# A two-batch encoder layer: held-back copies, other DRAM rows, low parts on one engine, longer score runs, and a list schedule that passes work over

## The chip, the cores and the metric

The kernel runs on one core of one Trainium2 chip. The metric is the device time of one execution in microseconds (us), as the median of several runs. A profiled execution gives the span (first to last instruction), the busy times of the engines and every instruction with its start.

The engines are TensorE (PE in the profile; its weight loads are PEld), VectorE (DVE), ScalarE (ACT), GpSimd (POOL) and SyncE (SP), which here issues all DMA transfers from one queue in program order.

## The reference

One layer of an encoder is applied to a prompt (512 tokens) and to a sample (1024 tokens) with the same weights, in float32, model width 1024. Cut to what matters:

```python
h = rmsnorm(x, norm_g)
qa, ka, va, za, qb, kb, vb, zb, ga, gb = split(h @ w_in)   # 4*512, 512,128,128,512, 1024,1024
qa, ka, qb, kb = (rmsnorm per head of 64)
oa = neighbourhood_attention(qa, ka, va, rpb_a) * silu(za)      # 8 heads, 8 x 16 window of the grid
ob = window_gqa_attention(qb, kb, vb, t5_table, sink_b) * silu(zb)  # 8 heads, 2 key heads, |i-j| <= 128
merged = sigmoid(ga) * (oa @ w_o_a) + sigmoid(gb) * (ob @ w_o_b)
y = x + merged @ w_out
```

## The kernel before

**Products.** Every float32 product is made of three float32r products. An operand is split into a high part (ACT copies it with rounding, line 1172) and a low part (the rest, by a subtraction on DVE or POOL, line 1177); the three products are high x high, high x low and low x high (lines 764 for the attention's projections, 1293 to 1295 elsewhere). The large products of the dense phases are partly done with Strassen-like sums of blocks: the sums of activations for the sample, called T, are made early, stored in the DRAM tensor `t_d`, read back at the start of the sample's dense phase into the tiles U, fh and w32, and split into the tiles T.

**Stages.** Normalization of the prompt; attention of the prompt; dense phase of the prompt, which also normalizes the sample; attention of the sample; dense phase of the sample. An attention phase runs six groups: four of branch A (two heads each) and two of branch B (four heads each). In a group each tile of 128 tokens (4 in the prompt, 8 in the sample) is projected with 24 products of 384 columns into a bank "p" of PSUM (two of these); squares are summed (`sq`, `ss`), POOL makes the factors (`rs_v`, `rs_r`, lines 795 and 802), DVE scales q and k (`qk`, line 819), PE transposes them (line 864) into a bank "x" (five of these). In group A the projection reads the activations directly; in group B it reads copies `hb` in another token order, four tiles of [128, 4, 128] a projection, made by ACT or DVE (lines 665 and 667).

`attend` collects blocks of 128 queries. A batch of them (two in A, one in B) is one operation of PE, the score run: for each block and pair of heads six products on 64 rows (line 937), two heads side by side on the two halves of the array, each head with its own "x" bank. `weigh` then adds bias and takes the maximum (line 972, DVE), the exponential (line 981, ACT), the scaling, transposes of the weights (line 1029), their split (`pp`) and the products with v (line 1066). The output tile `ot` goes to DRAM: in A one store of summed halves, in B two stores (one for each half e of the partitions) into `o_d[e, 4..7]` with 128 tokens in a row.

**Dense phases.** z products (`post_z` multiplies silu(z) with the attention's output read back from DRAM; for branch B two loads `ot`, added), gate products, the products with w_o and with w_out. Products that need nothing from the attention are also offered to PE during it: whole gate products on bank "d" (`fill_gates`, 3 in the prompt and 8 in the sample, in DRAM afterwards), and in the sample the first halves of four z products (`kept_z`, i = 0 to 3), where from i = 1 the second half waits for the attention's last exponential (`exps_done`).

**Order.** All operations are given to a planner (`Flow`) with the engines that may run them, estimated durations, a priority and what they wait for. A tile's work has the priority of its tile's number, the sample's attention 100 more; the next group's weights are three tiles ahead of their use, bias tables one. `run` is a list schedule: whenever an engine is free it takes the most urgent operation that is ready, has buffers, and would not be done sooner elsewhere; this fixes the order of instructions of each engine before the kernel is compiled. On the chip every engine goes through its list in order and waits on semaphores. In the sample's attention durations on ACT, DVE and POOL are planned 1.1 times longer (`slack`); the work of the dense phases has slack 1.

## Time and profile before

| | us |
|---|---|
| median of 3 runs | 1133.49 (1132.47 to 1138.85) |
| profiled execution, its own time | 1135.29 |
| its span | 1133.5 |
| PE busy | 1119.0 |
| DVE busy | 860.1 |
| ACT busy | 651.9 |
| POOL busy | 337.3 |

The granted clock of TensorE is 1.0 (its 2.4 GHz level) over the span. In the trace the prompt's attention ends at about 217 us, its dense phase at 400, the sample's attention at 787, its dense phase at the end. A matmul's row is its start and a modelled duration; since matmuls are pipelined, what one costs is read from the distance between starts. DMA share is the mean busy share of the core's 16 DMA engines.

### The profile page before, as it was taken

To read this page: it belongs to the slowest core of one execution; us is meant where nothing else is said; L and a number is where in the kernel's file an instruction comes from. 1 tells how busy PE (TensorE), PEld (TensorE's weight loads), DVE (VectorE), ACT (ScalarE), POOL (GpSimd) and SP (SyncE) were. 2 spreads that over 40 slices of the span, in tenths; PEclk is the share of its full clock that TensorE was granted. 3 is DMA by queue.
4 is the path that set the end of the run, shared out by engine and by line. 5 is a ranking of instruction groups with operands and counts; after the bars stand their busy time and mean duration, and the time that the engine had idled before them with its cause. 6 is when DMAs were issued, how large, how long until landed. Compare 5 with 4: busy or idle time off the path is not lost.

```text
span 1133.5 us, 18690 instructions
## 1 busy us (share of the span) xinstructions
PE 1119.0 (99%) x6079; PEld 973.2 (86%) x6079; DVE 860.1 (76%) x1988; ACT 651.9 (58%) x1499; POOL 337.3 (30%) x438
## 2 busy tenths in 40 slices
PE   8999999999999999999999999999999999999998
PEld 6999988888888889999999988988788888888887
DVE  5888797587776568787878888885988766677764
ACT  6777987644432257565769888876543335423430
POOL 4653433000011154434324344420333322222211
PEclk9999999999999999999999999999999999999999
DMA  7854543488886732121212314244977645867862
GB/s 263 276 155 138 184 115 103 110 257 248 256 278 216 254 128 91 27 63 30 82 41 85 81 38 112 57 131 121 307 241 234 224 156 170 281 207 222 280 215 93
DMA packets 139108, 186.11 MB, mean 164 GB/s; under 512 B 29897, under 2 KB 68561, under 8 KB 139010
## 3 DMA queue, kind: packets, MB, share of 16 engines
q1 hardware_dynamic: 139010, 184.91, 51.8%
q8 instruction: 48, 0.79, 0.3%
q14 instruction: 50, 0.41, 0.1%
HBM read 137.66 MB, written 51.92 MB: 167 GB/s over the span
## 4 chain that ended last, share of the span: by engine, by line
PE 93%; DMA 2%; DVE 2%; issue 1%; ACT 1%; POOL 1%; SPq 0%; DVEq 0%; ACTq 0%
PE p L764 25%; PE x L1294 9%; PE x L1295 9%; PE x L1293 9%; PE x L1066 5%; PE x L937 5%; PE x L1029 5%; PE d L1293 4%; PE d L1295 4%; PE d L1294 4%; PE p L1294 4%; PE p L1295 4%; PE p L1293 4%; PE x L864 2%; DMA w<-in_w_att_dram 1%
## 5 line engine op out<-in xcount | busy, mean ns | idle before, releaser
L764 PE MATMUL p<-whi,hh 128*128 128x384 f32 x384 | 133.4, 348 | 0.0
L764 PE MATMUL p<-whi,hl 128*128 128x384 f32 x384 | 132.2, 344 | 0.0
L764 PE MATMUL p<-wlo,hh 128*128 128x384 f32 x384 | 131.8, 343 | 0.0
L1172 ACT ACTIVATE whi<-raw 128x512 fp32r<-128x512 f32 (+1 forms) x140 | 81.4, 600 | 71.2 <-PE x L1294 22.3
L981 ACT ACTIVATE sb<-sb,mx 128x384 f32<-128x384 f32 (+1 forms) x192 | 107.8, 565 | 16.9 <-DVE mx L972 16.5
L1295 PE MATMUL x<-T,wlo 128*128 128x512 f32 x280 | 108.9, 389 | 0.0
L1294 PE MATMUL x<-T,whi 128*128 128x512 f32 x280 | 108.9, 389 | 0.0
L1293 PE MATMUL x<-T,whi 128*128 128x512 f32 x280 | 108.9, 389 | 0.0
L764 PE MATMUL p<-whi,hb 128*128 128x384 f32 x384 | 107.6, 346 | 0.0
L1177 POOL TENSOR_TENSOR wlo<-raw,whi 128x512 fp32r<-128x512 f32 (+1 forms) x33 | 39.5, 1204 | 215.6 <-DMA raw<-in_w_g_dram 112.9
L1040 DVE TENSOR_TENSOR pp<-x,pp 128x512 fp32r<-128x512 f32 (+1 forms) x136 | 82.5, 638 | 19.6 <-ACT pp L1035 19.0
L1177 DVE TENSOR_TENSOR wlo<-raw,whi 128x512 fp32r<-128x512 f32 (+1 forms) x107 | 72.0, 682 | 32.3 <-ACT whi L1172 28.7
L802 POOL TENSOR_TENSOR rs_r<-rs_v,mhalf 128x4 f32<-128x4 f32 (+1 forms) x72 | 80.5, 1118 | 5.7
L1035 ACT ACTIVATE pp<-x 128x512 fp32r<-128x512 f32 (+1 forms) x136 | 70.8, 559 | 15.8 <-PE x L1029 14.3
L1294 PE MATMUL x<-hl,whi 128*128 128x512 f32 x200 | 77.8, 389 | 0.0
L1295 PE MATMUL x<-hh,wlo 128*128 128x512 f32 x200 | 77.8, 389 | 0.0
L1293 PE MATMUL x<-hh,whi 128*128 128x512 f32 x200 | 77.8, 389 | 0.0
L1066 PE MATMUL x<-pp,v 128*128 128x256 f32 (+1 forms) x368 | 75.8, 322 | 0.0
L764 PEld LDWEIGHTS p<-whi,hl 128*128 128x128 f32 x384 | 72.6, 189 | 1.3 <-issue 1.0
L764 PEld LDWEIGHTS p<-wlo,hh 128*128 128x128 f32 x384 | 72.7, 189 | 1.0 <-issue 0.7
L764 PEld LDWEIGHTS p<-whi,hh 128*128 128x128 f32 x384 | 72.7, 189 | 0.7 <-DVE v L812 0.3
L764 PEld LDWEIGHTS p<-whi,hb 128*128 128x128 f32 x384 | 69.1, 188 | 3.1 <-issue 1.3
(388 smaller groups left out, 2965.1 us busy)
## 6 DMA issues: line engine op xcount, KB each, us to landing
raw<-in_w_g_dram SPq DMA_DIRECT2D x84, 256.0 KB
w<-in_w_att_dram SPq DMA_DIRECT2D x46, 384.0 KB
raw<-in_w_z_dram SPq DMA_DIRECT2D x40, 256.0 KB
ot<-o_d SPq DMA_DIRECT2D x36, 256.0 KB
g_d<-C SPq DMA_DIRECT2D x34, 256.0 KB
fr<-in_w_g_dram SPq DMA_DIRECT2D x28, 256.0 KB
raw<-in_w_out_dram SPq DMA_DIRECT2D x28, 256.0 KB
out_dram<-C SPq DMA_DIRECT2D x19, 256.0 KB
```

What stands on the lines that cost most here:

```text
L764: pe.matmul(ps.t[:, :GW], part[u](k), mv.t[:, c], start=k == 0 and m == 0, stop=k == KC - 1 and m == 2,)
L802: lambda e: nc.gpsimd.tensor_tensor(r.t[:, :nn], rv.t[:, :nn], mhalf[:, :nn], op=ALU.pow),
L937: pe.matmul(pss[2 * pair + i].t[:, :width], q.t[rows, u, at : at + P], kv[:, tiles[0] : tiles[-1] + 1 : step], start=n == 0, stop=n == 2,)
L981: act.activation(sb.t[:, :width], sb.t[:, :width], AF.Exp, bias=mx.t[:, i : i + 1], scale=-1.0, accum_out=sm.t[:, i : i + 1],)
L1035: lambda e, pt=pt, pp=pp, nn=nn: act.activation(pp.t[:, 0, :nn], pt.t[:, :nn], AF.Copy),
L1040: lambda e, pt=pt, pp=pp, nn=nn: dve.tensor_tensor(pp.t[:, 1, :nn], pt.t[:, :nn], pp.t[:, 0, :nn].bitcast(F32), op=ALU.subtract),
L1066: pe.matmul(out(), v.t[:, vs], mv(), start=first, stop=last)
L1172: (("act", ACT_(n)),), lambda e: act.activation(hi(), src(), AF.Copy), prio,
L1177: lambda e: engines[e].tensor_tensor(lo(), src(), hi().bitcast(F32), op=ALU.subtract), prio,
L1293: pe.matmul(out, hi.t[:, cs], mh(), start=first and k == 0, stop=False, **more)
L1294: pe.matmul(out, hi.t[:, cs], ml(), start=False, stop=False, **more)
L1295: pe.matmul(out, lo.t[:, cs], mh(), start=False, stop=last and k == len(ws) - 1, **more)
```

## The change

Six edits.

- Copies: the four `hb` copies of a B projection also wait until the projection six tiles earlier has begun. Only the first four of a phase were free to run earlier than that.
- DRAM rows: A outputs keep four rows of `o_d`; B outputs go to a new tensor `ob_d`, ordered as the z products read them. A load of 256 KB for the z product of B reads rows of 512 tokens (2 KB). In the sample each B block is stored with four transfers of pieces of 64 tokens (256 bytes) instead of two of 128 tokens (512 bytes); in the prompt the pieces keep their size.
- Low parts: for the sums read from `t_d` and the weights of the sample's first z pair (priority 0), the low parts are made on DVE only.
- Score runs: in the prompt's A groups a batch has four blocks instead of two, so it waits for the group's last tile. The second block of each two shares the banks of the first, at column 256.
- Late z products: the products of `kept_z` with i = 2 and 3 wait for the attention's last product with v (`f.weighed`).
- Patience: with `expect` the planner notes when each operation whose last input has been started will be ready. With `sooner` ACT, DVE and POOL pass over an operation with priority 90 or more and slack other than 1 (so the sample's attention) if an operation more urgent by over 3 will be ready within half its duration.

```diff
+PATIENT = ("act", "dve", "pool")
+URGENT = 3
+SHARE = 0.5
+FROM = 90
+AHEAD = 6
...
+        def expect(o, end):
+            for x in o.outs:
+                x.open -= 1
+                x.eta = max(x.eta, end + min(self.LAG.get((o.eng, e), 100) for e, _ in x.choice))
+                if not x.open and x.eta > now:
+                    coming[x.choice[0][0]].append(x)
+
+        def sooner(o, e, ns):
+
+            if e not in PATIENT or o.prio < FROM or o.slack == 1:
+                return False
+            coming[e] = [x for x in coming[e] if x.eta > now and x.eng is None]
+            t = [x.eta for x in coming[e] if x.prio < o.prio - URGENT and x.eta < now + SHARE * ns]
+            if t:
+                at(min(t), 4, None)
+            return bool(t)
...
-                        if all(room(v, n) for v, n in o.new) and not any(locked(v, e) or v.held and not v.t for v in o.vals) and not barred(o, e) and all(
+                        if all(room(v, n) for v, n in o.new) and not any(locked(v, e) or v.held and not v.t for v in o.vals) and not barred(o, e) and not sooner(o, e, ns) and all(
...
-    o_d = {geo.nt: dpool.tile([2, 8, P, geo.nt], F32, tag=f"o_d{geo.nt}", name=f"o_d{geo.nt}") for geo in (gp, gs)}
+    o_d = {geo.nt: dpool.tile([4, P, geo.nt], F32, tag=f"o_d{geo.nt}", name=f"o_d{geo.nt}") for geo in (gp, gs)}
+    ob_d = {geo.nt: dpool.tile([geo.nt // 512, 2, 8, 64, 512], F32, tag=f"ob_d{geo.nt}", name=f"ob_d{geo.nt}") for geo in (gp, gs)}
...
-                            prio - 1, new=[hb[m][q]], hold=[v], after=[o for u in h_ops.values() for o in u], port=True,
+                            prio - 1, new=[hb[m][q]], hold=[v], port=True,
+                            after=[*(o for u in h_ops.values() for o in u), f.begun[nt, prio - AHEAD]],
...
+            shared = br == "A" and nt == NT_P
...
-                pss = [bank("x") for _ in range(nh)]
+                second = shared and len(states) % 2
+                pss = [(v, 256) for v, _ in states[-1][2]] if second else [(bank("x"), 0) for _ in range(nh)]
...
+                                ps, a = pss[2 * pair + i]
                                 pe.matmul(
-                                    pss[2 * pair + i].t[:, :width], q.t[rows, u, at : at + P],
+                                    ps.t[:, a : a + width], q.t[rows, u, at : at + P],
...
+            f.weighed = o
...
-                for e in range(2):
-                    dst = o_d[nt][e, 4 + 2 * g : 6 + 2 * g, :, runs[0][0] : runs[0][0] + P]
-                    dst = dst.rearrange("c (i d) n -> d (c i) n", d=64)
...
+                m, t = 512 // nb, runs[0][0] // P
+                for n in range(nt // 512):
+                    for e in range(2):
+                        dst = ob_d[nt][n, e, 4 * g : 4 * g + 4, :, t * m : t * m + m].rearrange("a p m -> p a m")
+                        o = sp(
+                            lambda n=n, e=e, dst=dst: nc.sync.dma_start(dst, ot.t[e * 64 : e * 64 + 64, :, n * m : n * m + m]),
+                            1024 * m, prio, use=[ot],
+                        )
...
-                size = 2 if br == "A" else 1
+                size = 1 if br == "B" else 4 if nt == NT_P else 2
...
-        def split(hi, lo, src, n, prio, new_hi, new_lo, src_v, after=()):
+        def split(hi, lo, src, n, prio, new_hi, new_lo, src_v, after=(), both=True):
...
-                any_tt(n),
+                any_tt(n)[: 1 + both],
...
-                        (vh, k == 0), (vl, k == 0), [st],
+                        (vh, k == 0), (vl, k == 0), [st], both=d is m_d,
...
-            w = weight_tiles([*first, s2, s3, s1, raw[1, 1], s4], 6, prio - 0.5)
+            w = weight_tiles([*first, s2, s3, s1, raw[1, 1], s4], 6, prio - 0.5, prio > 0)
...
-                    src = o_d[nt][e, c].rearrange("p (i n) -> p i n", n=P)[:, :, a // nb : a // nb + m]
-                    dst = lambda ot=ot: ot.t[:, :n].rearrange("p (i n) -> p i n", n=m)
+                    src = ob_d[nt][a // nh, e].rearrange("(c i) p n -> c (i p) n", i=2)[c - 4, :, :n]
...
-            o = product(ps, ws[0], mov_h(0, 0), i / 4 - 1, True, True)
+            o = product(ps, ws[0], mov_h(0, 0), i / 4 - 1, True, True, [f.weighed] if i > 1 else [])
```

## Rows read from the trace of the kernel before

**Rows 1.** The page, part 1: busy us (share of the span) and instructions of each engine

```profile
PE 1119.0 (99%) x6079; PEld 973.2 (86%) x6079; DVE 860.1 (76%) x1988; ACT 651.9 (58%) x1499; POOL 337.3 (30%) x438
```

**Rows 2.** Busy by stretch: PE, PEld, DVE, ACT, POOL; then clock, DMA share, GB/s

```profile
600.00:650.00 50.00, 50.00 (x330) 45.57 (x328) 43.41 (x123) 45.85 (x106) 20.51 (x26) 1.00 0.28 80
...
800.00:820.00 20.00, 18.18 (x77) 13.76 (x75) 19.29 (x25) 11.06 (x21) 7.34 (x5) 1.00 0.96 308
```

**Rows 3.** Waits of PE over the span: us in total, times, longest us

```profile
PE x L864 <- DVE qk L819: 3.1, 3, 1.8
```

**Rows 4.** PE in order of time: start, us, line, tiles; round two score runs

```profile
63.43 0.34 PE L764 MATMUL p<-whi,hl 128*128 128x384 f32 x1
63.60 0.34 PE L764 MATMUL p<-whi,hh 128*128 128x384 f32 x1
63.87 0.97 PE L937 MATMUL x<-kt,qt 64*128 64x256 f32 x12
64.78 0.45 PE L764 MATMUL p<-wlo,hh 128*128 128x384 f32 x1
65.06 0.34 PE L764 MATMUL p<-whi,hl 128*128 128x384 f32 x1
...
740.31 1.33 PE L937 MATMUL x<-kt,q 64*128 64x384 f32 x12
```

**Rows 5.** Line 937 alone: count, duration ns min/median/max, first and last start; prompt's A

```profile
L937 PE MATMUL x<-kt,qt x96: 271/278/384, 38.5 to 127.6; 64*128 64x256 f32 x96
```

**Rows 6.** All engines in order of time, start of the sample's attention

```profile
402.23 1.31 POOL L1177 TENSOR_TENSOR fl<-fr,fh 128x512 fp32r<-128x512 f32 x1 [11.40 <-ACT fh L1172]
...
402.62 2.15 DVE L667 CAST hb<-hl 128x512 fp32r<-128x512 f32 x2
...
403.62 1.22 POOL L795 TENSOR_SCALAR rs_v<-ss 128x4 f32<-128x4 f32 x1
...
406.02 0.19 POOL L795 TENSOR_SCALAR rs_v<-ss 128x4 f32<-128x4 f32 x1
...
406.45 0.44 PE L864 MATMUL x<-ident,qk 128*128 128x128 f32 x2 [1.84 <-DVE qk L819]
```

**Rows 7.** Busy by stretch (columns as in rows 2), start of the sample's dense phase

```profile
796.00:798.00 2.00, 2.00 (x10) 1.65 (x10) 2.00 (x6) 1.97 (x5) 0.00 (x0) 1.00 1.15 296
...
804.00:806.00 2.00, 2.00 (x10) 1.69 (x9) 1.92 (x4) 2.00 (x5) 0.00 (x0) 1.00 1.01 371
```

**Rows 8.** SP's issues in order of time, end of the attention and after

```profile
785.75 1.24 SPq L1102 DMA_DIRECT2D o_d<-ot__10494  x2
...
793.90 3.66 SPq L1520 DMA_DIRECT2D u_d<-C  x1
...
804.60 3.58 SPq L1520 DMA_DIRECT2D u_d<-C  x1
```

**Rows 9.** DVE and POOL in order of time, low parts of T and of weights

```profile
805.83 0.69 DVE L1177 TENSOR_TENSOR T<-w,T 128x512 fp32r<-128x512 f32 x1
...
810.76 1.71 POOL L1177 TENSOR_TENSOR wlo<-raw,whi 128x512 fp32r<-128x512 f32 x1
811.27 1.75 DVE L1177 TENSOR_TENSOR T<-w,T 128x512 fp32r<-128x512 f32 x1
```

**Rows 10.** PE in order of time, T products of the first z pair

```profile
811.11 0.40 PE L1293 MATMUL d<-T,whi 128*128 128x512 f32 x1
813.08 0.50 PE L1294 MATMUL d<-T,whi 128*128 128x512 f32 x1 [1.57 <-DVE T L1177]
...
820.67 0.50 PE L1294 MATMUL p<-T,whi 128*128 128x512 f32 x1 [0.65 <-DVE T L1177]
```

**Rows 11.** PE in order of time, end of the sample's attention

```profile
784.00 1.10 PE L1066 MATMUL x<-pp,v 128*128 128x512 f32 x4
...
786.32 0.39 PE L1293 MATMUL x<-hh,whi 128*128 128x512 f32 x1
786.54 0.39 PE L1294 MATMUL x<-hl,whi 128*128 128x512 f32 x1
```

More of the change, by code (lines that the diff above doesn't have):

```diff
@@ L137 @@
 class Op:
-    __slots__ = ("choice", "emit", "new", "vals", "after", "outs", "prio", "left", "lag", "key", "eng", "port")
+    __slots__ = ("choice", "emit", "new", "vals", "after", "outs", "prio", "left", "lag", "key", "eng", "port", "slack", "open", "eta")
 class Flow:
@@ L210, in run @@
         for o in self.ops:
-            o.left = len(o.after)
+            o.left = o.open = len(o.after)
+            o.eta = 0
             for a in o.after:
@@ L258, in barred @@
             return True
+        coming = {e: [] for e in ready}
+        def expect(o, end):
[12 more added lines that the diff above has]
+            return bool(t)
         def backlog(e, item):
@@ L300, in run @@
                         at(dma_free + 950, 2, got)
+                    expect(got, dma_free + 950 if got.lag else now + ns)
             if not events:
@@ L947, in attend @@
             o = f.op(
-                (("pe", ns),), emit, prio, new=[v for _, _, pss, sbs in states for v in (*pss, *sbs)],
+                (("pe", ns),), emit, prio, new=[v for _, _, pss, sbs in states for v in (*(ps for ps, a in pss if not a), *sbs)],
                 use=[queries(block) for block in batch], after=[o for b in batch for t in b[1] for o in info[t][2]],
@@ L967, in weigh, with score, emit @@
             mx, sm, rs, es = sums
-            def score(i, ps, sb):
-                def emit(e, i=i, ps=ps, sb=sb):
+            def score(i, ps, a, sb):
+                def emit(e, i=i, ps=ps, a=a, sb=sb):
                     init = 3.0e38 if br == "A" else nsink[:, 4 * g + i : 4 * g + i + 1]
                     dve.tensor_tensor_reduce(
-                        out=sb.t[:, :width], in0=ps.t[:, :width], in1=bias_of(br, nb_t, i, table), scale=1.0,
+                        out=sb.t[:, :width], in0=ps.t[:, a : a + width], in1=bias_of(br, nb_t, i, table), scale=1.0,
                         scalar=init, op0=ALU.add, op1=ALU.min, accum_out=mx.t[:, i : i + 1],
@@ L990, in score @@
                 x.vals = [*x.vals, mx]
-            for i, (ps, sb) in enumerate(zip(pss, sbs)):
-                score(i, ps, sb)
+            for i, ((ps, a), sb) in enumerate(zip(pss, sbs)):
+                score(i, ps, a, sb)
             if br == "B":
@@ L1088, in emit @@
                     if len(runs) == 1:
-                        dst = over(o_d[nt][0, g], runs).rearrange("(i p) n -> p i n", i=2)
+                        dst = over(o_d[nt][g], runs).rearrange("(i p) n -> p i n", i=2)
                         nc.sync.dma_start(dst, ot.t[:64, ::2])
@@ L1092, in emit @@
                     for i in range(2):
-                        dst = over(o_d[nt][0, g, 64 * i : 64 * i + 64], runs)
+                        dst = over(o_d[nt][g, 64 * i : 64 * i + 64], runs)
                         nc.sync.dma_start(dst, ot.t[:64, 2 * i].rearrange("p (a b) -> p a b", b=64))
@@ L1258, in load_raw, with weight_tiles @@
             return v
-        def weight_tiles(operands, per, prio):
+        def weight_tiles(operands, per, prio, both=True):
             n = -(-len(operands) * 4 // per)
@@ L1275, in weight_tiles @@
                         lambda src=src, sc=sc: src.t[:, sc], m * P, prio,
-                        (hi, ti not in seen), (lo, ti not in seen), [src],
+                        (hi, ti not in seen), (lo, ti not in seen), [src], both=both,
                     )
@@ L1529, in post_z @@
                 if c < 4:
-                    src, dst = o_d[nt][e, c, :, a : a + n], lambda ot=ot: ot.t[:, :n]
+                    src = o_d[nt][c, :, a : a + n]
                 else:
-                    src = o_d[nt][e, c].rearrange("p (i n) -> p i n", n=P)[:, :, a // nb : a // nb + m]
-                    dst = lambda ot=ot: ot.t[:, :n].rearrange("p (i n) -> p i n", n=m)
+                    src = ob_d[nt][a // nh, e].rearrange("(c i) p n -> c (i p) n", i=2)[c - 4, :, :n]
                 dma(
-                    lambda dst=dst, src=src: nc.sync.dma_start(dst(), src), 512 * n, prio - 0.5, new=[ot],
+                    lambda ot=ot, src=src: nc.sync.dma_start(ot.t[:, :n], src), 512 * n, prio - 0.5, new=[ot],
                     after=o_stores[c, a // nh],
```

9 lines of the change are left out of this document (2 added, 7 removed).

## The prediction

> **What bounds the kernel now.** I began with the busy shares of the page: TensorE (PE) is busy 1119.0 of 1133.5 us [rows 1]. The profiled execution took 1135.29 us, 1.8 us more than its span, and the median of the runs is 1133.49 us; I take the sum in the span and subtract it from the median. In the stretch 600 to 650 us, the second half of the sample's attention, PE is busy 50.00 of 50, with ScalarE (ACT) at 45.85 and VectorE (DVE) at 43.41 [rows 2]: the code gives PE products there that nobody waits for yet (gate products on the bank "d", then the first z products), and they fill every gap. So moving DVE or ACT work changes nothing by itself. Only two things shorten this kernel: fewer PE cycles, or less of the 14.5 us in which PE stands still.
>
> Where does it stand still? The change can reach two causes: in the list of waits the transposes of line 864 wait for `qk` of line 819, 3.1 us in three places, longest 1.8 [rows 3], and in the order of time a product stands 1.57 us at once for the low part of a T sum (line 1177) [rows 10]. The head, waiting for its first loads, and the drain at the end hold most of the rest and are not touched. The stretch 800 to 820 shows PE at 18.18 of 20 while the DMA engines are at 0.96 and DVE at 19.29 [rows 2]: this is the start of the sample's dense phase, where the stored sums T are read from DRAM.
>
> **The change part by part.**
>
> Score runs. The score products (line 937) work on 64 rows, all others on 128. The last 128-row product before a run starts at 63.60, the run at 63.87, the next product at 64.78 and the one after at 65.06 [rows 4]. Undisturbed neighbours start 0.17 us apart (63.43, 63.60). From 63.60 to 65.06 are 1.46 us; two ordinary starts take 0.35 of it, so the run costs 1.11. How much of that is switching? A run of the same 12 products with 384 columns takes 1.33 where 256 columns take 0.97 [rows 4]: 0.36 for six concurrent pairs of 128 more columns, 0.06 a pair, so 256 columns are worth 0.12 a pair and six pairs 0.72. What is left, 0.39, is the way in and out of the mode. The prompt's A groups hold 96 such products [rows 5], eight runs of 12. Four blocks in one batch make four runs of 24. Gain 4 x 0.39 = **1.6 us** of PE time. Ends: 1.6, and nothing if the bunching makes as much idle time: the run now waits for the fourth tile, then eight score operations come to DVE at once, and four of the five "x" banks are held twice as long. The cover is the next group's projections (two "p" banks) and the gate products; I take 1.6, since PE is never idle in that part of the trace.
>
> Copies. The B projections read a copy of the activations (`hb`, four buffers). Nothing keeps the first four copies of a phase from running as soon as an engine is free, and in the sample they do so at 402 us: DVE takes two from 402.62, 2.15 us [rows 6]. They are first read in group B, four A groups later. Beside them POOL's `rs_v` of the first A tile takes 1.22 us, where the next one, with no copy beside it, takes 0.19. It sits on the chain ss, rs_v, rs_r, qk, and PE waits for it until 406.45, idle 1.84 [rows 6]. Held back until the projection six tiles earlier has begun, the copies run in the fourth A group instead, where PE does not wait for ACT or DVE. Gain 1.22 - 0.19 = **1.0 us**. Ends: 1.84, if the second tile's chain, delayed by ACT's copies, is part of the wait; nothing, because POOL is also busy with a gate weight's low part until 403.54 [rows 6] and a new order can put more there. In the prompt they go the same way, from a place where PE is covered: nothing.
>
> DRAM rows. For z columns of branch B in the sample, each load of `o_d` gathers 1024 pieces of 256 bytes, two loads a product. In the stretch 796 to 798, where these pass, the DMA engines move 296 GB/s at a share of 1.15; in 804 to 806 371 at 1.01 [rows 7]: 257 against 367 per full share. A load of 256 KB thus costs 1.02 instead of 0.71 us; as rows of 2 KB each saves 0.3. Four pass before the last T load: 1.2 us of a saturated DMA. And directly behind each such pair SP sits in the issue of one small store for 3.66 and 3.58 us [rows 8], with the T loads (U, fh, w) queued behind; without the small pieces this block should go. Against it: the stores of the last B block become four issues instead of two, and two cost 1.24 us [rows 8]. The T loads stand behind them on SP, so they start 1.24 later. For the first T sums these two about cancel: 0. For the last four T loads, issued behind the second block, two blocks of 3.6 are gone: they are no longer late, and the waits for the parts made of them go, 1.2 us in two late starts, the last at 820.67 with 0.65 of idle [rows 10].
>
> Low parts. In the sample's first z pair, and for the T sums, POOL may take low parts. While POOL runs one (1.71 at 810.76), DVE's T low part takes 1.75, where an undisturbed one takes 0.69 [rows 9]; PE waits for exactly this one: it starts a product at 811.11 and the next only at 813.08 [rows 10], 1.97 instead of 0.22 [rows 11], a loss of 1.75. With all on DVE, behind 808.4 there are five low parts (two more T, the two weights that POOL had, and T's last) of 0.69: 3.45, or 4.1 with the `ot` sum between; T's last ends at 811.8 to 812.5 instead of 813.02. Gain 0.5 to 1.2, I take 0.8.
>
> Together the dense start has 1.75 + 1.4 (three further late starts between 809 and 821, the last of them the one at 820.67) = 3.1 us to give; from the two edits I take 0.8 + 1.2 = **2.0 us**. Ends: 3.1, and nothing if PE only runs into the next missing operand, DVE being at 19.29 of 20.
>
> Late z products. Products i = 2 and 3 now wait for the last value product of the attention. Before, that product is at 784.00 and the first of i = 2 already follows it, at 786.32 [rows 11]. So the edit moves nothing in the old order: 0. It only keeps them as cover for the T loads should the order change.
>
> Patience. In the sample's attention an ACT, DVE or POOL operation is passed over if one at least three tiles more urgent is to be ready within half its duration. It shortens the chains that free banks, but PE is covered there (50.00 of 50 [rows 2]), so what it gains comes out only as fill kept for the dense start, already counted to its end. Ends: 1 us gained, and 1 lost in idle slices; I take 0.
>
> Sum: 1.6 + 1.0 + 2.0 = 4.6 us of 1135.29, so 1130.7 for a profiled execution, and **1128.9 us** as median.
>
> **The rivals.**
>
> 1. Only the mode switches are saved. The dense start stays bound by DMA (shares 1.15 and 1.01 [rows 7]) and DVE, and the wait for `qk` moves to another operation. For it: one late operand there is followed by the next in the rows. Against: SP's two blocks are plainly from the small pieces. 1133.49 - 1.6 = 1131.9.
>
> 2. All that can close closes: 1.6 + 1.84 + 3.1, and 0.9 of the other `qk` waits: 7.4, so 1126.1. For it: fill exists at each place; against: a new order has small waits of its own.
>
> 3. Slower: fill runs out before the attention ends. Before, all z products not held back were used up at 786.32, 1.4 us after the last value products, which start at 784.00 and take four starts of 0.23 [rows 11]. Holding back i = 2 and 3 takes 10.6 us (48 products of 0.22) away from that cover. If patience leaves ACT or DVE (43 to 46 of 50 [rows 2]) idle for 0.35 us twice in each of the group B tiles, 16 tiles, the chain grows 11.2, PE stands 9.8, and 4.6 is given back: 1138.7. It is slower than before from a growth of 6.0 us on. Against it: weights, bias tables and the first copies are nearly the only operations three tiles ahead.
>
> 4. The small stores bite. Each B block of the sample now stores 256-byte pieces. With the 1.24 us of issue not cancelled and 0.3 for the slower rate of such pieces, T is late by 1.5: gain 3.1, 1130.4. The Trainium skill, page "DMA: Bandwidth & Descriptors", section Specifications, wants at least 512 bytes for line rate and names a read-modify-write below it, which speaks against this edit. The trace of before shows 256-byte pieces as loads only, and no row can show what a store of them costs.
>
> **How the numbers follow.** Forecast 0.46 (1128.9, own range 1126.8 to 1131); rivals 1 to 4: 0.22, 0.14, 0.08, 0.10. The range for 8 in 10 goes from rival 2's side, 1125.5, to past rival 1 with one microsecond or two of new waits, 1134.5; rival 3 is left out. A measurement of this kernel tells about 0.5% from no change, 5.7 us. Faster by more: rival 2 and a third of the forecast, 0.30. Slower by more: over half of rival 3, 0.05. Within: 0.65.
>
> **What the profile after should show.** Prompt score runs of 24 products, four of them, with the same 0.39 around each. No `hb` copy near 402; `rs_v` there at 0.19; PE's wait for `qk` at that place 0.8 or less. No SP issue over 2 us near 794 and 805; loads of `ob_d` with 2 KB rows; four B stores a block. No T low part on POOL, T low parts of 0.69 on DVE, and PE idle in 800 to 825 falling from 2.5 to under 1 us. PE's busy time lower by 1.6 at most. I am wrong if PE shows idle time before the last value product (rival 3), if its idle time is 13 us or more in spite of the steps (rival 1), or if new waits stand in the prompt between 38 and 110 us, where the runs come late.

## The result and the profile after

The changed kernel takes 1140.22 us (median; 1137.51 to 1144.49) where the kernel before took 1134.79 beside it: 1.0050 times as long, 95% interval 1.0032 to 1.0068. It is slower by half a per cent, 5.7 us past the upper end of the range that was given. The profiled execution took 1140.18 us, with a span of 1138.4.

The page, part 1, of the kernel after: busy us, share of the span, instructions.

```profile
PE 1122.7 (99%) x6079; PEld 975.0 (86%) x6079; DVE 855.7 (75%) x1955; ACT 657.2 (58%) x1505; POOL 362.3 (32%) x465
```

Beside [rows 1] two numbers went the wrong way: PE is busy 3.7 us longer though it has less to switch, and POOL 25 us longer though low parts were taken from it. PE's 3.7 is no work: a product that starts at the lower clock, or right behind a wait, is shown longer (0.63 or 0.50 us instead of 0.39 in the rows at 820 to 822 below), and PE's work, taken from its starts, is 1.4 us lower (table below). So busy time does not tell where the loss is; waits and late starts do.

The waits of PE in the kernel after, without the first loads' 4.3 us in the head: operand and who made it, us in total, times, longest us.

```profile
...
PE p L1326 <- DVE T L1209: 2.6, 1, 2.6
PE d L1326 <- DVE T L1209: 2.1, 4, 0.7
PE d L1325 <- ACT fc L1647: 1.4, 3, 0.7
PE p L1325 <- ACT whi L1204: 0.6, 1, 0.6
PE x L892 <- DVE qk L847: 0.5, 1, 0.5
...
```

(Lines have moved: 1325 to 1327 are the three products that were 1293 to 1295, 1209 is the low part that was 1177, 892 and 847 the transposes and `qk` that were 864 and 819, 968 the score run that was 937.) The waits for `qk`, 3.1 us in [rows 3], are 0.5. In their place stand 4.7 us of waits for one thing, the low parts of the T sums on DVE, which the change had put on DVE so that they should come sooner.

Busy time by stretch in the kernel after (columns as in rows 2):

```profile
800.00:820.00 20.00, 15.88 (x65) 11.52 (x63) 19.80 (x22) 9.66 (x19) 12.50 (x8) 1.00 0.75 275
...
818.00:821.00 3.00, 0.41 (x2) 0.37 (x3) 2.97 (x4) 1.52 (x3) 1.98 (x1) 1.00 0.31 87
821.00:825.00 4.00, 4.00 (x12) 3.16 (x11) 3.26 (x6) 0.67 (x2) 0.00 (x0) 0.57 0.18 66
```

In 800 to 820 PE falls from 18.18 to 15.88 of 20 and POOL rises from 7.34 to 12.50 [rows 2], while the DMA share falls from 0.96 to 0.75: the DMA side did get better (275 GB/s at a share of 0.75 are 367 per full share, before 308 at 0.96, 321). What PE waits for is on DVE, which is busy 19.80 of 20, a part of it with operations that take longer than alone. The last line is the price behind the long wait: the granted clock is 0.57 for four microseconds, near the lower of its two levels (1.2 GHz), and products start 0.43 us apart (the last two rows of the next list) instead of 0.23.

DVE and POOL in order of time in the kernel after, the PE product that waits, and two of those behind it (start, us, engine, line, tiles; in brackets the idle time before and its cause):

```profile
815.30 1.51 DVE L1209 TENSOR_TENSOR wlo<-S,whi 128x256 fp32r<-128x256 f32 x1
816.74 2.11 DVE L1198 TENSOR_TENSOR C<-C,ot 128x512 f32<-128x512 f32 x1
818.77 0.67 DVE L1198 TENSOR_TENSOR C<-U,d 128x512 f32<-128x512 f32 x1
819.37 1.17 DVE L1209 TENSOR_TENSOR T<-U,T 128x512 fp32r<-128x512 f32 x1
...
814.97 1.56 POOL L1198 TENSOR_TENSOR S<-raw 128x512 f32<-128x512 f32 x1 [1.34 <-DMA raw<-in_w_z_dram]
816.61 1.35 POOL L1198 TENSOR_TENSOR S<-S,raw 128x512 f32<-128x512 f32 x1
817.92 2.06 POOL L1198 TENSOR_TENSOR S<-raw 128x512 f32<-128x512 f32 x1
...
820.59 0.50 PE L1326 MATMUL p<-T,whi 128*128 128x512 f32 x1 [2.62 <-DVE T L1209]
...
821.46 0.63 PE L1326 MATMUL x<-T,whi 128*128 128x512 f32 x1
821.89 0.63 PE L1327 MATMUL x<-T,wlo 128*128 128x512 f32 x1
```

The chain is to be read backwards. PE stands 2.62 us for the T part that DVE starts at 819.37; that part comes behind two DVE operations of 1.51 and 2.11 us which alone take 0.42 and 0.69; and each of the slow ones has a `tensor_tensor` of POOL beside it, making weight sums S for the next pair of z products, which nobody waits for yet. When POOL's 817.92 + 2.06 = 819.98 is over, the T part needs 0.56 more, about its own time. The one operation in between that is not slowed, `C<-U,d` at 818.77 with 0.67, reads one of its inputs from PSUM. The Trainium skill, page "SBUF — State Buffer", section "SBUF: two separate sides", states it as a lock that a POOL operation and a DVE operation with two SBUF inputs hold in turn; these rows agree with it.

**Where the time went.** PE's late starts, by stretch, in microseconds. A late start is the distance of a PE instruction from the one before it, less the median distance for that pair of kinds over all traces of this study; PE's work is the time from its first to its last instruction less its late starts. 30 to 380 is the prompt, 380 to 415 the change to the sample's attention, from 783 on its dense phase; behind 850 it is -0.4 nearly everywhere. How finely kinds are told apart moves a whole column by one to three microseconds, all kernels alike, so only differences within a column are used.

| kernel | 0-30 | 30-380 | 380-415 | 415-783 | 783-850 | PE's work | time against before |
|---|---|---|---|---|---|---|---|
| before | 7.0 | 0.9 | 2.2 | 2.6 | 3.6 | 1109.2 | 1 |
| after | 6.1 | 3.5 | 1.6 | 3.0 | 8.7 | 1107.8 | 1.0050 |
| low parts marked | 6.5 | 3.6 | 0.9 | 3.0 | 2.9 | 1107.8 | 0.9998 |
| low parts on both | 6.0 | 3.8 | 0.0 | 3.4 | 3.5 | 1107.8 | 1.0008 |
| rows back | 6.9 | 3.7 | 1.3 | 3.0 | 5.8 | 1107.8 | 1.0041 |
| no patience | 5.3 | 3.5 | 2.2 | 3.5 | 6.3 | 1107.6 | 1.0054 |
| score runs alone | 7.3 | 3.9 | 2.6 | 2.8 | 3.9 | 1107.7 | 1.0018 |
| copies alone | 5.8 | 2.0 | 2.6 | 3.0 | 4.8 | 1109.1 | 1.0036 |
| low parts alone | 6.7 | 0.9 | 2.3 | 2.6 | 5.3 | 1109.2 | 1.0021 |
| low parts alone, marked | 6.1 | 1.9 | 5.8 | 2.4 | 3.5 | 1109.2 | 1.0005 |
| rows alone | 6.3 | 2.3 | 2.2 | 1.9 | -0.1 | 1109.2 | 0.9981 |
| rows, low parts marked | 7.2 | 1.7 | 2.6 | 2.5 | 2.3 | 1109.2 | 0.9991 |
| before, other estimate | 6.4 | 3.4 | 4.5 | 2.5 | 1.4 | 1109.3 | 1.0034 |
| after, other estimate | 6.0 | 12.7 | 0.0 | 2.3 | 8.1 | 1107.7 | 1.0100 |
| rows alone, other estimate | 6.2 | 2.1 | 1.6 | 2.7 | 3.8 | 1109.3 | 1.0018 |
| marked, copies in sample only | 7.1 | 4.8 | 0.9 | 3.0 | 2.3 | 1107.8 | 1.0009 |
| sample's rows | 6.5 | 0.8 | 3.2 | 2.5 | -0.1 | 1109.2 | 0.9977 |
| sample's rows and copies | 5.7 | 2.3 | 2.0 | 2.4 | 0.7 | 1109.2 | 0.9983 |
| old rows, new order | 5.9 | 1.7 | 4.6 | 1.9 | 4.0 | 1109.2 | 1.0021 |
| new rows, old order | 6.0 | 1.0 | 3.1 | 2.1 | 2.1 | 1109.2 | 1.0004 |

The dense start alone, 8.7 - 3.6 = 5.1, is the loss; about 1.6 of it is the fallen clock. The score runs are worth 1.4 to 1.6 us of work in each kernel that has them, and the prompt gives back 2.6. The table also warns. Eight kernels have the very same order of instructions on the four compute engines up to 780 us: before, the two with low parts alone, rows alone, rows with low parts marked, sample's rows, and the last two. In single executions their late starts in 380 to 415 are 2.2, 2.3, 5.8, 2.2, 2.6, 3.2, 4.6 and 3.1, and in 30 to 380 they run from 0.8 to 2.3. Differences of up to 3.6 us in the one column and 1.5 in the other say nothing by themselves.

### The profile page after: what moved, and what is told of

The parts are those of the page before. It is cut to its first block, busy times and chain, and to the rows that moved or that the text cites. A ratio compares the mean times of both kernels' runs of the same rounds, so it can differ in the third digit from the quotient of the medians.

```text
span 1138.4 us, 18738 instructions
## 1 busy us (share of the span) xinstructions
PE 1122.7 (99%) x6079; PEld 975.0 (86%) x6079; DVE 855.7 (75%) x1955; ACT 657.2 (58%) x1505; POOL 362.3 (32%) x465
## 4 chain that ended last, share of the span: by engine, by line
PE 89%; DMA 4%; DVE 3%; issue 1%; ACT 1%; SPq 1%; POOL 1%; ACTq 0%; POOLq 0%; DVEq 0%
PE p L792 26%; PE x L1327 8%; PE x L1326 8%; PE x L1325 8%; PE x L1097 5%; PE x L1060 5%; PE x L968 5%; PE d L1325 4%; PE d L1326 4%; PE d L1327 4%; PE p L1326 4%; PE p L1325 4%; PE p L1327 4%; PE x L892 2%; DMA raw<-in_w_out_dram 1%
## 5 line engine op out<-in xcount | busy, mean ns | idle before, releaser
L1209 POOL TENSOR_TENSOR wlo<-raw,whi 128x512 fp32r<-128x512 f32 (+1 forms) x35 | 42.4, 1218 | 218.9 <-ACT whi L1204 210.5
L792 PE MATMUL p<-whi,hb 128*128 128x384 f32 x384 | 110.0, 348 | 0.0
```

What stands on the lines that cost most here:

```text
L792: pe.matmul(ps.t[:, :GW], part[u](k), mv.t[:, c], start=k == 0 and m == 0, stop=k == KC - 1 and m == 2,)
L1209: lambda e: engines[e].tensor_tensor(lo(), src(), hi().bitcast(F32), op=ALU.subtract), prio,
```

## The experiments

**The lost mark.** The planner gives each operation a mark, `port`, if no other is set by hand: `{"dve", "pool"} <= {e for e, _ in choice}`. It never plans two marked operations, one on DVE and one on POOL, beside each other. An operation that only DVE may run has not both engines in its choice, so `any_tt(n)[: 1 + both]` took the mark away from the low parts. Theory A: this is the loss. Theory B: the loss comes with the new DRAM rows and their four stores. The first kernel is the changed one with one word more:

```diff
-                use=src_v, after=[a, *after], **{...},
+                use=src_v, after=[a, *after], port=True, **{...},
```

> The changed kernel, with the DVE-only low parts marked again as users of what DVE and POOL share (the planner keeps marked operations of the two engines apart; an operation that only DVE may run lost the mark). Theory A (the lost mark lets POOL sums run beside the T low parts, which then take 1.2 to 2.1 us instead of 0.68 and make PE wait): PE's late starts between 786 and 850 fall from 8.7 us to 5 or less, the clock stays full, and the time falls by 3 us or more against the changed kernel, to about 1.002 of the kernel before. Theory B (the four stores at the attention's end hold up the T loads): no more than 1 us better, 1.004 to 1.005. Theory C (any new plan has its own waits): anywhere within 3 us, with waits in other places.

1134.92 us, ratio 0.9998 (0.9987 to 1.0009): the whole loss is gone with the mark. Late starts at the dense start 2.9, clock 1.0 throughout. The T parts of line 1209 made from U on DVE in 800 to 825 (those made from fh and w are left out here), count and duration ns min/median/max, in the kernel after:

```profile
L1209 DVE TENSOR_TENSOR T<-U,T x6: 677/924/1783, 803.7 to 821.8; 128x512 fp32r<-128x512 f32 x6
```

and with the mark:

```profile
L1209 DVE TENSOR_TENSOR T<-U,T x6: 682/684/1765, 803.8 to 817.8; 128x512 fp32r<-128x512 f32 x6
```

The median is down to the undisturbed 0.68, the last starts 4.0 us earlier. A maximum of 1.77 remains: the mark keeps two operations apart in the plan, not on the chip, where one that comes late can still meet the other.

The T parts are not the whole of it. Over all DVE's operations of 128x512 and 128x256 in 800 to 822, the time above the undisturbed 0.68 and 0.42 is 7.6 us in the kernel after, 5.3 before and 3.6 with the mark; of this the T parts have 3.9, 3.5 and 1.6. So DVE and POOL met before the change too, and the meetings that the change added fell mostly on the operations ahead of the T parts, as 1.51 and 2.11 in the rows above.

Low parts on both engines again, all else of the change kept:

```diff
-                any_tt(n)[: 1 + both],
+                any_tt(n),
```

> The changed kernel with the low-part edit undone: POOL may take T and first-pair low parts again. Theory A: the mark is back, so late starts between 786 and 850 fall to 3 to 5 us and the time to 1.001 to 1.003 of the kernel before. Theory B: T stays late by the stores, late starts stay at 7 or more, 1.004 or more. My own sum of before, by which DVE alone is the better place, would make it worse than the changed kernel by 0.8 us.

1.0008 (0.9995 to 1.0022), late starts at the dense start 3.5. This edit undone, the loss is gone too, and what is left of the change is no gain.

The rows and stores as before, all else of the change kept:

```diff
-    ob_d = {...[geo.nt // 512, 2, 8, 64, 512]...}
+    ob_d = {...[2, 4, P, geo.nt]...}   # two stores a block, loads gather 64-token pieces
```

> The changed kernel with the old DRAM rows: two stores of 512-byte pieces a B block, loads of 256-byte pieces. Theory B: the first T load is issued 1.2 us sooner after the last value product, ACT's first silu 2 us sooner, and PE's late starts between 786 and 850 fall by 2 us or more; SP blocks of 3.6 us come back. Theory A: DVE and POOL still meet, late starts stay at 7 to 10 us and the time at 1.004 to 1.007. My sum of before has the rows as a gain of 1.2 us, so undoing costs that.

1.0041 (1.0025 to 1.0056) beside 1.0050 (1.0032 to 1.0068). Most of the loss stays without the new rows, so they are not its cause. Late starts at the dense start are 5.8 against 8.7; that a part of the loss needs the new rows is not excluded by this pair.

No patience:

```diff
-            if e not in PATIENT or o.prio < FROM or o.slack == 1:
+            if True:
```

> The changed kernel without patience: the list schedule passes over nothing. If patience costs (rival 3 of the prediction): late starts in the sample's attention, 1.9 us between 600 and 786, fall below 1 and the time falls by more than 1 us. If it does nothing, as I took it: the time stays within 1 us of the changed kernel, late starts between 786 and 850 stay at 7 us or more. Theory C: up to 3 us either way, from waits in other places.

1.0054 (1.0036 to 1.0072): the step that gave the change its name is worth nothing that can be measured, as was predicted.

**Each edit alone on the kernel before.** Score runs:

```diff
-                size = 2 if br == "A" else 1
+                size = 1 if br == "B" else 4 if nt == NT_P else 2
```

> The kernel before with the longer score runs of the prompt alone. The accounting of late starts puts PE's work 1.4 us lower in every kernel with this edit, and the stalls of 30 to 220 us 1.7 higher (two waits for a weight copy, fc, at 125 and 146 us). Theory P (the runs themselves bring those waits, since a batch of four blocks makes its DVE and ACT work arrive in one lump): PE's work -1.4, stalls of the prompt's attention about 2.8 instead of 1.06, in all 1134.7 to 1135.0 beside 1135.0 before. Theory Q (the waits come from another edit): stalls stay at about 1.1 and the kernel gains the whole 1.4, 1133.5.

1.0018 (1.0006 to 1.0031): theory P by its mechanism, though it had set the waits equal to the gain, and the kernel is slower. The work is 1.5 us less, but 30 to 380 us holds 3.9 of late starts instead of 0.9. PE and POOL in order of time in this kernel:

```profile
65.38 0.44 PE L864 MATMUL x<-ident,qk 128*128 128x128 f32 x2 [1.79 <-DVE qk L819]
...
59.06 1.78 POOL L698 TENSOR_TENSOR bias<-mask,raw 128x128 f32<-128x128 f32 x5
60.81 2.03 POOL L1180 TENSOR_TENSOR fl<-fr,fh 128x512 fp32r<-128x512 f32 x1
62.92 0.78 POOL L795 TENSOR_SCALAR rs_v<-ss 128x4 f32<-128x4 f32 x1
63.79 1.07 POOL L802 TENSOR_TENSOR rs_r<-rs_v,mhalf 128x4 f32<-128x4 f32 x1
```

It is the wait of [rows 6] at another place: POOL has 3.8 us of bias and gate weights in front of the factors of the tile that PE wants next. My word in the expectation, "one lump of DVE and ACT work", does not describe it; the new order does.

Copies held back:

```diff
-  ... after=[o for u in h_ops.values() for o in u], port=True,
+  ... port=True, after=[*(o for u in h_ops.values() for o in u), f.begun[nt, prio - AHEAD]],
```

> The kernel before with the held-back copies alone. If the prediction's step on them is right: rs_v near 403 us at about 0.2 us and PE's wait for qk of 2.0 us there gone to 0.8 or less, so the stalls of 380 to 415 us fall from 2.2 to about 1, in all 1134.0. If the copies also bring the waits for fc in the prompt's attention (theory Q of the score-run kernel): stalls of 30 to 220 us near 2.8 and no net gain, 1135.5.

1.0036 (1.0022 to 1.0050), slower. The copies are gone from 402, PE's wait for `qk` there is 0.62, but ACT's `whi` now keeps PE 0.9 at 383, and the dense start loses 1.2; the prompt's 1.1 more is within what one order shows. Its profiled execution took 1137.02 where the median is 1138.99, so the stretches account for only half of these 4 us, and the rest is not shown. The hold acts in the prompt too, where the first four copies ran at 31 us and now run at 79 to 84; I had costed that at nothing.

Low parts on DVE only, without and with the mark:

> The kernel before with low parts on DVE only, and nothing else. Theory A (an operation that only DVE may run loses the planner's mark for the port shared by DVE and POOL, so POOL's sums are put beside it and it takes 1.2 to 2.1 us instead of 0.68): T low parts of 1.2 us and more in 800 to 825, POOL there above 10 us (7.34 before), stalls of 783 to 850 us from 3.6 to 7 or more, 1138.5 to 1140.5. Theory B (the loss needs the new DRAM rows, which let the operands come in another order): stalls of 783 to 850 stay under 4.5, 1135 to 1136.

> The kernel before with low parts on DVE only and the port mark set by hand. Theory A: low parts at 0.7 us each, none on POOL, nothing of POOL's tensor_tensor beside them; stalls of 783 to 850 at 2.8 to 3.6 us, 1134.2 to 1135.0 (the prediction's 0.8 us for this step at best). Theory B: the same as the kernel with the low parts alone. If DVE alone is simply too slow for all low parts, stalls of 783 to 850 stand at 4.5 or more with the low parts at 0.7, 1136 and up.

1.0021 (1.0010 to 1.0033) and 1.0005 (0.9989 to 1.0021). The order of these two is that of the kernel before up to the dense start, so they show the step by itself: 5.3 and 3.5 beside 3.6. The T parts made from U, without and with the mark:

```profile
L1177 DVE TENSOR_TENSOR T<-U,T x6: 680/946/1767, 802.8 to 819.2; 128x512 fp32r<-128x512 f32 x6
...
L1177 DVE TENSOR_TENSOR T<-U,T x7: 677/684/693, 800.1 to 821.5; 128x512 fp32r<-128x512 f32 x7
```

Theory A holds, at less than its size: I expected 7 or more. And with the mark the step brings nothing; I had counted 0.8 for it.

DRAM rows and four stores a block, alone, and with marked low parts on DVE:

> The kernel before with the new DRAM rows and the four stores a block alone. The prediction's step: SP's blocks of 3.6 us gone, the T operands of the fourth block of rows 1.2 us earlier, so stalls of 783 to 850 us 2.4 instead of 3.6, 1134.4 beside 1135.5 before. Rival (the late end of four stores): the attention's last stores land 2 us later and the first operand of the second z products with them, stalls of 783 to 800 up by 0.9 and no net gain, 1135.5 to 1136.

> The kernel before with new DRAM rows, and low parts on DVE only with the port mark set by hand: all that the change does at the dense start, without its reshuffling of the prompt. Theory A (the dense start is right once the mark is there): stalls of 783 to 850 at 2.9 or less, as in the changed kernel with the mark, prompt as before, 1134.5. If nothing is gained there even so: stalls of 783 to 850 at 3.5, 1135.5.

0.9981 (0.9971 to 0.9992): this edit alone makes the kernel faster, and the late starts of the dense start, 3.6, vanish altogether. With the low parts on DVE, mark and all, 2.3 of them are back and the ratio is 0.9991 (0.9981 to 1.0001). That suggests that POOL is needed there; the two intervals overlap, so it is not shown.

**How much is the plan?** One estimate of the planner changed, nothing else:

```diff
-            ns = 396 + sum(nh // 2 * 3 * PE_(places(block)[2]) for block in batch)
+            ns = 436 + sum(nh // 2 * 3 * PE_(places(block)[2]) for block in batch)
```

> The kernel before with one estimate of the planner changed and nothing else: a score run is planned 40 ns longer. The chip computes the same with the same instructions, in another order. Theory C (any new plan has its own waits, of some 1 to 3 us, because the planner does not know what an operation really takes beside others): stalls of 30 to 380 us differ from 0.9 by 1 us or more to one side, the time is 1133.5 to 1138.5. Theory D (the plan is robust, and waits come from the edits themselves): stalls within 0.5 us in each stretch, 1135.0 to 1136.0.

1.0034 (1.0020 to 1.0049): theory C, with a time somewhat past its range. The same work in another order is slower by two thirds of what the whole change costs. So a change of this kernel that reaches the planner early is, besides what it does, a draw of a new order. To tell the two apart I put the change, and the rows alone, under that other estimate:

> The whole change under that other estimate. If the lost mark is a property of the edit and not of one plan: low parts of 1.2 us and more beside POOL in 800 to 825 again, stalls of 783 to 850 at 4 or more, and slower than the kernel before of 1134.4, 1138 to 1142. If it was an accident of one plan: stalls of 783 to 850 under 3, 1134 to 1137.

> The new DRAM rows (alone) under the other estimate of the planner (score runs 40 ns longer), to be set beside the kernel before under that estimate (1139.3, stalls of 783 to 850 us 1.45). If the rows' gain is their own (SP no longer blocked, so loads issue earlier): stalls of 783 to 850 at 0.5 or less, and faster than 1139.3 by 1 us or more. If the gain of the rows alone was a lucky plan: stalls of 783 to 850 as likely up as down, 2 to 4 us, and no gain on 1139.3.

The whole change: 1.0100 (1.0080 to 1.0121), 1146.57 us, well past what I expected, with 8.1 at the dense start where the kernel before has 1.4 under this estimate. DVE's T parts there, as above:

```profile
L1209 DVE TENSOR_TENSOR T<-U,T x6: 679/958/1780, 805.7 to 820.4; 128x512 fp32r<-128x512 f32 x6
```

The slowed low parts come again under another order. How much of the 8.1 is the lost mark was not measured: no kernel with the mark was run under this estimate, and the rows alone have 3.8 there. (Another 9 us of late starts in the prompt are this order's own, by an estimate some 3 of them a fall of the clock at 361 us, taken from the distances of the products behind it.) The rows alone: 1.0018 (1.0005 to 1.0031) against 1.0034, intervals that overlap, and 3.8 at the dense start against 1.4. There the rows bring no gain at that place.

The changed kernel with the mark, and the copies held back in the sample only:

> The changed kernel with the port mark, and the copies held back in the sample's attention only. If the held-back copies of the prompt cause the waits there (fc at 126 and 147 us): stalls of 30 to 220 us near 1.5 instead of 3.2, 380 to 415 still at 0.9, 1133.2, faster than before by 0.2%. If the longer score runs cause them: 30 to 220 us at 3 or more, as with the score runs alone (4.1), 1135 to 1136.

1.0009 (0.9997 to 1.0021). The waits in the prompt grew to 4.8 us, the same two for `qk` as with the score runs alone (2.0 and 1.7 us late at 65.6 and 76.0; with the score runs alone 2.0 and 1.2 at 65.4 and 75.4). So the score runs bring waits by themselves; in the kernel after, the copies held back in the prompt changed which operation is late, not that one is.

**Edits kept to the sample.** I wanted the prompt to keep its order: new rows in the sample only, and with the copies held back there as well.

```diff
-            else:
+            elif nt == NT_P:
                 for e in range(2):   # two stores into o_d, as before
...
+            else:                    # four stores into ob_d, as in the change
```

> The kernel before with the new rows in the sample only. As the prompt's plan does not change, stalls of 30 to 415 as before (3.1) and those of 783 to 850 tell the rows alone: at 0 to 1 if unblocking SP closes the dense start, 1131; at 2.4 by the prediction's term of 1.2, 1133.2; at 3.6 if the gain of the rows in both phases was a lucky plan, 1134.4.

> The kernel before with the new rows in the sample only and the copies held back in the sample only; score runs, low parts, patience and late z products as before. If confined edits gain without touching the prompt: stalls of 30 to 380 as before (0.9), of 380 to 415 at 0.9 instead of 2.2, of 783 to 850 at 0 to 1 instead of 3.6, so 4 us less: 1130.5, the best so far. If the plan after them loses it again: 1133 to 1135.

0.9977 (0.9965 to 0.9988) and 0.9983 (0.9970 to 0.9996). The first is 2.6 us faster than before by its ratio. But it is no new kernel in its order: the planner sees two stores a block in the prompt either way, so the rows alone had left the prompt's order as it was, and the two kernels have the same order on the four compute engines from start to end. 0.9981 and 0.9977 are two measurements of one order, and they agree. The dense start of the kernel with the sample's rows, busy time by stretch, and its T parts on DVE:

```profile
800.00:825.00 25.00, 25.00 (x112) 20.70 (x111) 24.19 (x38) 12.10 (x23) 9.27 (x5) 1.00 0.79 282
...
L1189 DVE TENSOR_TENSOR T<-U,T x5: 685/691/693, 799.4 to 815.4; 128x512 fp32r<-128x512 f32 x5
```

PE is never late, and the sixth T part of this kind is on POOL. Holding the copies back adds nothing to it.

**Rows or order?** The new rows change the order too: in the sample the planner sees four stores where it saw two. The two mixed cases separate them. One has the order of the last kernel and old rows; the other the order of the kernel before on all four compute engines, and new rows (two stores for the planner, issued as four):

> The order of the kernel with the sample's new rows (four stores a block), every engine the same, but the old rows: each load for the B products again gathers 1024 pieces of 256 bytes. If the rows themselves gain: SP is blocked for 3.6 us near 794 and 804 us again and stalls of 783 to 850 us are back at 2.5 to 4, 1134 to 1135. If the order gains: stalls of 783 to 850 at 0 to 1 in spite of the blocks, 1132 to 1133.

> The mirror case: the order of the kernel before on TensorE, VectorE, ScalarE and GpSimd, and the sample's new rows (the planner sees two stores a block, each issued as two transfers). If the rows themselves gain: no SP block, stalls of 783 to 850 at 2.4 (the prediction's 1.2) or less, 1131 to 1133.5. If the order gains: stalls of 783 to 850 at 3 to 4 as before, 1134 to 1135.

Late starts in 783 to 850:

| | old order | new order |
|---|---|---|
| old rows | 3.6 | 4.0 |
| new rows | 2.1 | -0.1 |

By these single executions the rows are worth 1.5 under the old order and 4.1 under the new one; the new order with the old rows is worth nothing and the kernel is slower, 1.0021 (1.0011 to 1.0031). SP's issues with old rows under the new order:

```profile
795.54 2.08 SPq L1546 DMA_DIRECT2D ot<-o_d  x2
797.67 3.09 SPq L1531 DMA_DIRECT2D u_d<-C  x1
...
809.24 2.94 SPq L1531 DMA_DIRECT2D u_d<-C  x1
```

with new rows under this same order (the kernel with the sample's rows):

```profile
795.27 0.40 SPq L1532 DMA_DIRECT2D u_d<-C  x1
...
804.25 0.32 SPq L1532 DMA_DIRECT2D u_d<-C  x1
```

and in the kernel after, with new rows and its own order:

```profile
784.85 2.57 SPq L1135 DMA_DIRECT2D ob_d<-ot__10507  x4
...
793.23 0.98 SPq L1566 DMA_DIRECT2D ot<-ob_d  x2
794.26 0.87 SPq L1552 DMA_DIRECT2D u_d<-C  x1
...
803.93 0.32 SPq L1552 DMA_DIRECT2D u_d<-C  x1
```

The blocks follow the small pieces and not the order. New rows with the old order come out at 1.0004 (0.9991 to 1.0017), so in whole executions the 1.5 us are not resolved; they are seen in the profile alone.

## Why the prediction was wrong, by its steps

- **Score runs, 1.6:** PE's work fell by 1.4 to 1.6, and the run is now 1.6 us for 24 products. Kernel after, PE in order of time:

```profile
67.63 0.34 PE L792 MATMUL p<-whi,hl 128*128 128x384 f32 x1
67.89 1.69 PE L968 MATMUL x<-kt,qt 64*128 64x256 f32 x24
69.51 0.44 PE L792 MATMUL p<-whi,hh 128*128 128x384 f32 x1
```

  The term was right, its cover was not. I took 1.6 "since PE is never idle in that part of the trace". That holds for the old order. With four blocks in a batch the order is a new one, and 2.6 to 3.9 us of waits came into the prompt. The text named new waits between 38 and 110 us as a sign of being wrong, and gave them no price. With the score runs alone they stand there, at 65 and 75; in the kernel after they stand later, at 125, 146 and 355.
- **Copies, 1.0:** the mechanism was right, the size is not shown. In the kernel after, the wait for `qk` there is gone, and POOL's row is

```profile
400.94 0.19 POOL L823 TENSOR_SCALAR rs_v<-ss 128x4 f32<-128x4 f32 x1 [24.31 <-DVE ss L816]
```

  Over the nine kernels that hold the copies back in the sample, 380 to 415 holds 1.3 us of late starts on average; over the eleven others 3.2, but eight of these share one order, in which single executions differ by up to 3.6. The direct pairs are 2.6 against 2.2 (copies alone) and 2.0 against 3.2 (in the sample only). And the edit as written also holds the prompt's copies back, which the sum put at nothing: alone it is slower by 4 us, of which the stretches show half.
- **DRAM rows, 1.2:** the mechanism is shown: SP's blocks and the late T loads went. The size, 1.5 us in the case with the old order, is from one execution of each kernel, and the whole times do not resolve it (1.0004).
- **Small stores (rival 4):** issue takes 2.57 us instead of 1.24 [rows 8], as that rival reckoned, and the first T load starts at 789.51 instead of 788.18 before. No price of this is seen behind it: with the old order the dense start still gains. The packets of the trace give the slower rate that it reckoned with: between 640 and 783 us a packet of 256 bytes takes 25.8 ns on average and one of 512 bytes, in the kernel before, 41.4 ns, so the 256 KB of one block hold the 16 DMA engines 1.65 us instead of 1.32, 0.3 more, and nothing waited for it. What is behind the slower rate the packets do not tell. That the trace of before has 256-byte pieces as loads only was wrong: the prompt's A stores of line 1094 have them too.
- **Low parts, 0.8:** this is the step that failed. I set the new low parts at 0.69 each, the duration of one with nothing of POOL beside it, because POOL would have no low parts any more. POOL's other work was not counted: the sums S and low parts for the next pair of z products stood next, and POOL, free, took them as they became ready. And the planner's rule that kept DVE and POOL apart was tied to the very choice that the edit removed. I listed DVE at 19.29 of 20 [rows 2] as a reason why nothing might be gained, and gave the step no end below nothing, though the row that I used, 1.75 beside POOL's 1.71 [rows 9], is the price of exactly this meeting. Alone it costs 1.7 us of late starts, in the whole change 5.2 to 5.8 (8.7 against 3.5 or 2.9).
- **The clock:** not in the sum at all. The wait of 2.62 us was followed by products at 0.43 instead of 0.23 for 3.4 us, 1.6 us more. It is not most of the loss: of the ten executions of the kernel after, three kept the full clock on average, and they took 1137.51, 1139.14 and 1139.22, still longer than the 1134.79 before.
- **Late z products and patience, 0 each:** patience alone was tested, and is nothing. Rival 3 did not come: from 415 us to the last value product PE is idle for 0.4 us in all, before for 1.0. The hold on the z products was not tested by itself.
- **The rivals:** the slower side had one mechanism, the fill that runs out, at 0.08. That "a new order has small waits of its own" stood under rival 2 as a remark. It should have been a rival with a price: the kernel before with one other estimate is 3.9 us slower.
- **The base:** the sum starts from 1133.49, the median of three runs. Beside the change the kernel before took 1134.79, so 1.3 of the 11.3 us between forecast and measurement are the base's, and no step's.

## What to carry to other kernels

When an edit takes a choice away from an operation, look up what else was derived from that choice; here a safety rule against two engines meeting hung on it, and one word gave back the whole loss, 5 to 6 us. Cost an operation that is moved to a busy engine at the duration it has beside its neighbour, not alone, and ask what the engine that was relieved does next. Where a planner makes the order, measure what an idle change of one estimate does before believing an effect of that size, and measure each edit alone: the new rows gain about 0.2% by themselves (0.19 and 0.23, twice the same order), and with the rest of the change around them, mark and all, nothing.

## What was not expected of the hardware

- A POOL operation can be the one that waits: with DVE running operations back to back, one low part on POOL took 3.72 us instead of 1.28, and DVE's beside it 0.69 each. Kernel with the sample's rows, in order of time:

```profile
807.22 3.72 POOL L1189 TENSOR_TENSOR wlo<-S,whi 128x512 fp32r<-128x512 f32 x1 [31.14 <-ACT whi L1184]
810.90 1.28 POOL L1189 TENSOR_TENSOR T<-U,T 128x512 fp32r<-128x512 f32 x1
...
807.88 0.69 DVE L1189 TENSOR_TENSOR T<-fh,T 128x512 fp32r<-128x512 f32 x1
808.49 0.69 DVE L1189 TENSOR_TENSOR T<-U,T 128x512 fp32r<-128x512 f32 x1
...
809.69 0.69 DVE L1178 TENSOR_TENSOR U<-fr,x 128x512 f32<-128x512 f32 x1
```

  POOL's operation ends at 810.94, 1.25 us after DVE starts the first one with an input in PSUM (`x`), which is about POOL's own time. In the kernel after it was DVE that waited, also with operations back to back; what decides which of the two loses is not shown.
- The length of PE's idle time does not settle whether the clock falls. It fell in or right behind idle times of 2.62 us (after), 2.75 (after, other estimate), 2.68 (low parts alone, marked) and 2.04 (old rows, new order), and did not with 1.84 (before), 2.00 (score runs alone) and 2.36 (new rows, old order). The shortest of the first and the longest of the others stand at the same place. For each of the two kernels, old rows with the new order first, the product behind the idle time, and the stretch behind it (columns as in rows 2, the clock is the third number from the end):

```profile
407.17 0.44 PE L864 MATMUL x<-ident,qk 128*128 128x128 f32 x2 [2.04 <-DVE qk L819]
409.00:413.00 4.00, 3.91 (x16) 3.41 (x16) 3.02 (x11) 0.63 (x2) 0.78 (x1) 0.63 0.16 49
...
406.64 0.44 PE L865 MATMUL x<-ident,qk 128*128 128x128 f32 x2 [2.36 <-DVE qk L820]
409.00:413.00 4.00, 4.00 (x25) 4.00 (x24) 2.77 (x10) 1.18 (x4) 1.07 (x3) 1.00 0.18 49
```

  What makes the difference stays open.
